# Turning two units a group through DRAM in a short attention branch, and moving six weight subtractions to GpSimd

## The chip, the cores and the metric

The kernel runs on one core of one Trainium2 chip. The metric is the device time of that core in microseconds (us) for one launch, the median of the runs shown. The engines are TensorE (PE in the profile, with PEld for its weight loads), VectorE (DVE), ScalarE (ACT), GpSimd (POOL) and SyncE (SP, which here only issues DMAs). Each takes its instructions in the order of its own queue and waits on semaphores for the others.

## The reference

One encoder layer runs over two sequences with the same weights: `x_sample` with 512 tokens and `x_prompt` with 1024, both 1024 wide, in float32. The token mixer has two branches that are merged by gates:

```python
z = xn @ w_in
qa, ka, va, qb, kb, vb, ga, gb = jnp.split(z, idx, axis=-1)
qa = _apply_rope(_rmsnorm(qa..., q_norm_g), cos, sin)      # 8 heads
ka = _apply_rope(_rmsnorm(ka..., k_norm_g), cos, sin)      # 2 key heads, 4 query heads each
o_a = _gqa_attention(qa, ka, va)                           # branch A: softmax(q k^T / 8) v, all tokens
o_b = _neighbourhood_attention(qb, kb, vb, rpb)            # branch B: windows of 8 x 16 tokens
merged = sigmoid(ga) * (o_a @ w_proj_a) + sigmoid(gb) * (o_b @ w_proj_b)
x = x + merged @ w_out
x = x + square(relu(rmsnorm(x) @ w_up)) @ w_down
```

A last RMS norm follows. The change touches branch A of the short sequence and the first weights of branch B of the long one.

## The kernel before

**Numbers in two parts.** Products are made in a float32 form that TensorE reads at one pass, and the lost precision is made up by splitting. A value is copied by ScalarE into a high part (`split`, line 203; `AF.Copy` into `F32R`), and the low part is the value less the high part, a subtraction (line 210) by the engine that `subtract[0]` names: VectorE, or GpSimd where it is set so. A product is then two or three matmuls (`mm3`, line 220).

**Order of the work.** `run` handles the short sequence first (`NB` = 1, `NT` = 4 tiles of 128 tokens), then the long one (`NB` = 2, `NT` = 8), then comes the MLP. Within a sequence: for each of two groups of four heads a phase R (projection, norm, rotation of q, k, v; tiles `z`, `zv`, `pq`) and a phase A (attention); then phase B (branch B), phase G (merge and output projection). The program is written in one order; a planner sorts each engine's queue from it by its own costs, and grants buffers as older tiles come free, so that the queues need not have the program's order.

**Phase A.** A unit is a head and a block of 512 queries; a short group has four units, a long one eight. For each 128 queries, `s_tile` makes the scores in PSUM (`s`, lines 810 and 811, pool `big` with two buffers), VectorE takes the maximum (line 813), and ScalarE the exponential (line 822) into `p`, queries on partitions. The product with the values needs keys on partitions, and there are two ways to turn `p`:
- On TensorE: `t_chunk` transposes four blocks of 128x128 into PSUM (`pT`, line 857); ScalarE makes the high part `pth` from PSUM (line 860) and VectorE the low part `ptl` (line 861).
- Through DRAM: the exponential is written with its columns permuted, VectorE transposes 32x32 blocks in place (line 875, `turn_a`), SP stores the tile (`ta`, line 876) and fetches it in quarters in the turned order (`hq`, `fetch_a`, line 901); ScalarE makes the high part (line 906) and GpSimd the low part in two halves (line 908, `cut_a`).

Before the change, the long sequence sends every second unit of a head (`qb` = 1) through DRAM; the short one transposes all units on TensorE. `pv` (lines 844 and 845) multiplies with the values, `LAG` = 2 chunks behind the turning; `finish_o` scales and stores the result.

**Filling.** `fill` holds matmuls of a gate (`gps`, 24 of them a column chunk, weights `w_g`) that are put between the attention's own by `fill.pull`. In the long sequence's phase A `subtract[0]` is GpSimd, and it is set back to VectorE at its end (line 974).

**Start of phase B.** `prep(0)` asks for the value strips and the bias; the gate 3328 is added to `fill` (line 1315); `load_qk(0)` (line 1316) loads and splits the first query and key weights (`w_bq`, `w_bk`); one pull (line 1317) starts the gate, which loads and splits its first chunk of weights; then `qkproj` (line 1318) multiplies (`pqb`, `pkb`).

Of the kernel before, what the change touches and what calls it, by code (L numbers as in the profile page):

```python
# [18 lines left out]
P = 128  # L19
# [42 lines left out]
def encoder(ctx: ExitStack, tc: tile.TileContext, xs, outs, w):  # L62
# [24 lines left out]
    def slot(shape, dt, name, left=False):  # L87
        return (s8l if left else s8r).tile(shape, dt, tag="s8", name=name)
# [336 lines left out]
    def run(tr, nxt, first):  # L425
# [120 lines left out]
        for g in range(2):  # L546
# [251 lines left out]
            with phase(f"phA{N}_{g}") as ph:  # L798
                units = [(h, qb) for h in range(4) for qb in range(NB)]
                PP, L4, rd = {}, {}, {}  # L800

                def s_tile(u, j):
                    h, qb = u
                    nm = f"{N}_{g}_{h}_{qb}_{j}"
# [48 lines left out]
                def t_chunk(u, kc):  # L853
                    h, qb = u
                    pt = mm(f"pT{N}_{g}_{h}_{qb}_{kc}")
                    for j in range(4):
                        nc.tensor.transpose(pt[:, j * P : (j + 1) * P], PP[u, j][:, kc * P : (kc + 1) * P], ident)
                    hi = ph.tile([P, 512], F32R, tag="pth", name=f"pth{N}_{g}_{h}_{qb}_{kc}", bufs=3)
                    lo = ph.tile([P, 512], F32R, tag="ptl", name=f"ptl{N}_{g}_{h}_{qb}_{kc}", bufs=3)
                    nc.scalar.activation(hi, pt, AF.Copy)  # L860
                    nc.vector.tensor_tensor(lo, pt, hi.bitcast(F32), op=ALU.subtract)
                    queue.append((u, kc, hi, lo))
# [25 lines left out]
                def fetch_a(u, i):  # L888
                    nm = f"{N}_{g}_{u[0]}_{i}"
                    if i < 3:  # L890
                        hl = slot([P, 2, 16, 64], F32R, f"hq{nm}")
                        hi, lo = hl[:, 0], hl[:, 1]
                    else:
                        hi, lo = (
                            ph.tile([P, T], F32, tag="P", name=f"hq{nm}_{e}", bufs=8)
                            .bitcast(F32R)
                            .rearrange("p (a w) -> p a w", w=64)
                            for e in range(2)
                        )
                    src = PD[u].rearrange("t (a i) (b w) -> i b (t a) w", i=32, b=4)[:, :, :, 64 * i : 64 * i + 64]  # L900
                    nc.sync.dma_start(lo.bitcast(F32), src)
                    quarter[u, i] = hi, lo

                def cut_a(u, i):
                    hi, lo = quarter[u, i]
                    nc.scalar.activation(hi, lo.bitcast(F32), AF.Copy)
                    for a in (slice(0, 8), slice(8, 16)):
                        nc.gpsimd.tensor_tensor(lo[:, a], lo[:, a].bitcast(F32), hi[:, a].bitcast(F32), op=ALU.subtract)

                if NB == 2:  # L910
                    subtract[0] = nc.gpsimd
# [6 lines left out]
                    for h in range(4):  # L918
# [15 lines left out]
                        for kc in range(NT):  # L934
# [6 lines left out]
                            hi, lo = (t[:, :, kc % 2 * 32 : kc % 2 * 32 + 32] for t in quarter[u, kc // 2])  # L941
                            queue.append((u, kc, hi, lo))
                            fill.pull(0 if kc in (1, 4) else 1)
                            next_pv()
                            if h < 3 and kc in (4, 6):
                                fetch_a(nd, kc // 2 - 2)
                else:
                    for j in range(4):
                        ends = s_tile(units[0], j)
                        last_exp[:] = [ends]  # L950
                        fill.pull(2)
                    for ui, u in enumerate(units):
                        h, qb = u
                        if first:
                            bias_row(g * 4 + ui)
                            if g == 0 and ui == 1:
                                early["a"] = load_a(1)
                            if g == 0 and ui == 2:
                                early["v"] = load_v(1, slot)
                        nxt_u = units[ui + 1] if ui + 1 < len(units) else None  # L960
                        sdone = 0
# [98 lines left out]
        with phase(f"phB{N}") as ph:  # L1060
# [1057 lines left out]
```

## Time and profile before

| | us |
|---|---|
| median of 3 runs | 2098.93 |
| lowest, highest run | 2098.87, 2101.75 |
| the profiled execution | 2099.86 |
| its span, first to last instruction | 2098.1 |

The profile is one execution. Its mean granted TensorE clock is 0.996. A row of a timeline gives the start, the time taken, the engine, the line, the operation, what is written and read, the shape, and in brackets the idle time ahead of it with what ended that. A row of a group or of a tile gives the shortest, the median and the longest in nanoseconds. In a row of windows, each engine's busy time is followed by its count of instructions; the last three numbers are the granted clock, the DMA engines' mean share and GB/s. Matmuls overlap, so a record's time (0.39 us for 512 columns) is longer than the spacing from one to the next.

### The profile page before, as it was taken

What the parts mean: (1) busy time and instruction counts of PE and PEld (TensorE: products, weight loads), DVE (VectorE), ACT (ScalarE), POOL (GpSimd) and SP (SyncE); (2) the same over time, 40 slices, a digit from 0 to 9 for tenths busy, and PEclk for the clock granted to TensorE, in tenths of its full rate; (3) what the DMA queues carried; (4) which work ended last, traced back from release to release, by engine and by line L of the source; (5) the groups of instructions that cost most, each with busy time, mean ns of one, the idle gap of its engine ahead of it and who ended that gap; (6) DMA issues with size and microseconds to landing.
All of it is one profiled execution on the core that took longest, in us unless ns stands there. A gap on an engine that the chain in (4) does not pass through costs nothing. (4 is left out here: it accounts for less than half of the span.)

```text
span 2098.1 us, 31227 instructions
## 1 busy us (share of the span) xinstructions
PE 2070.3 (99%) x10615; PEld 1815.6 (87%) x10615; DVE 1468.7 (70%) x2697; ACT 1142.8 (54%) x2455; POOL 441.3 (21%) x550
## 2 busy tenths in 40 slices
PE   9999999999999899999999999999999999999998
PEld 8888778888898788888888999999999988888887
DVE  6665786778458746778845777787777777669563
ACT  6674653668557735556413566565656634334442
POOL 2323310317725733453002000011000000000000
PEclk9999999999999999999999999999999999999999
DMA  6537557558528767776544556487445899688461
GB/s 194 148 111 207 158 163 256 186 147 228 152 67 230 197 169 206 218 243 200 192 170 155 182 188 210 145 252 208 149 157 161 284 339 350 214 279 279 151 210 62
DMA packets 407910, 409.99 MB, mean 195 GB/s; under 512 B 98367, under 2 KB 334919, under 8 KB 407751
## 3 DMA queue, kind: packets, MB, share of 16 engines
q1 hardware_dynamic: 368119, 339.16, 52.5%
q10 hardware_dynamic: 29408, 41.96, 5.9%
q0 software_dynamic: 10224, 26.88, 5.0%
q8 instruction: 84, 1.38, 0.3%
q14 instruction: 75, 0.61, 0.1%
HBM read 294.21 MB, written 114.49 MB: 195 GB/s over the span
## 5 line engine op out<-in xcount | busy, mean ns | idle before, releaser
L216 PE MATMUL dn<-wd,ah 128*128 128x512 f32 x1248 | 384.1, 389 | 0.0
L216 PEld LDWEIGHTS dn<-wd,ah 128*128 128x128 f32 x1248 | 234.2, 188 | 48.4
L216 PE MATMUL dn<-wd,al 128*128 128x512 f32 x624 | 242.8, 389 | 0.0
L1592 ACT ACTIVATE ah<-ar 128x512 fp32r<-128x512 f32 x168 | 104.6, 628 | 207.4 <-PE dn L216 198.1
L216 PE MATMUL gpss<-xs_0h,w_gs 128*128 128x512 f32 x512 | 186.6, 401 | 0.0
L1593 DVE TENSOR_TENSOR al<-ar,ah 128x512 fp32r<-128x512 f32 x168 | 114.6, 688 | 81.7 <-ACT ah L1592 69.2
L216 PE MATMUL ud<-B,A 128*128 128x384 f32 x768 | 145.0, 337 | 2.3 <-DVE c L1710 2.3
L216 PE MATMUL uc<-B,A 128*128 128x384 f32 x768 | 143.7, 334 | 0.0
L216 PE MATMUL ua<-B,A 128*128 128x384 f32 x768 | 139.1, 334 | 0.0
L216 PEld LDWEIGHTS dn<-wd,al 128*128 128x128 f32 x624 | 117.1, 188 | 24.5
L216 PEld LDWEIGHTS ud<-B,A 128*128 128x128 f32 x768 | 135.1, 189 | 2.6 <-DVE c L1710 2.6
L216 PEld LDWEIGHTS ua<-B,A 128*128 128x128 f32 x768 | 134.1, 188 | 0.2
L216 PEld LDWEIGHTS uc<-B,A 128*128 128x128 f32 x768 | 134.0, 188 | 0.2 <-ACT A L1592 0.2
L180 POOL TENSOR_TENSOR rs_f<-ms_f,mhalf 128x1 f32<-128x1 f32 x6 | 4.0, 667 | 590.7 <-DVE ms_f L176 590.7
L813 DVE TENSOR_REDUCE nms<-ss 128x1 f32<-128x1024 f32 (+1 forms) x96 | 99.3, 1037 | 32.2 <-PE ss L811 32.0
L216 PE MATMUL ops<-wh_os,mgs 128*128 128x512 f32 x384 | 119.5, 391 | 0.0
L822 ACT ACTIVATE ps<-ss,nms 128x1024 f32<-128x1024 f32 (+1 forms) x96 | 93.3, 973 | 37.4 <-DVE nms L813 36.3
L216 PEld LDWEIGHTS gpss<-xs_0h,w_gs 128*128 128x128 f32 x512 | 96.6, 189 | 17.8
L216 PE MATMUL gpss<-xs_0l,w_gs 128*128 128x512 f32 x256 | 101.4, 396 | 0.0
L1592 ACT ACTIVATE A<-S 128x512 fp32r<-128x512 f32 x128 | 75.8, 623 | 32.7 <-DVE S L1655 23.9
L216 PE MATMUL gpss<-xs_1h,w_gs 128*128 128x512 f32 x256 | 91.3, 395 | 0.4 <-ACT sgs L470 0.4
L1225 POOL TENSOR_SCALAR pbs<-pbs,rlbs 128x384 f32<-128x384 f32 (+1 forms) x96 | 71.7, 752 | 84.7 <-DVE rlbs L1224 70.4
(307 smaller groups left out, 5170.3 us busy)
## 6 DMA issues: line engine op xcount, KB each, us to landing
ar<-ud SPq DMA_DIRECT2D x120, 512.0 KB, 4.9
br<-in_w_mlp_down_dram SPq DMA_DIRECT2D x72, 512.0 KB, 5.4
rawu<-in_w_mlp_up_dram SPq DMA_DIRECT2D x64, 512.0 KB, 4.2
ud<-c ACTq DMA_DIRECT2D x128, 192.0 KB, 3.8
raw_gs<-in_w_in_dram SPq DMA_DIRECT2D x32, 512.0 KB, 3.9
tas<-ps SPq DMA_DIRECT2D x32, 512.0 KB, 3.7
hqs<-tas SPq DMA_DIRECT2D x32, 512.0 KB, 5.3
ud<-cs SPq DMA_DIRECT2D x64, 192.0 KB
```

The costliest lines, as they stand in the source:

```text
L180: op = nc.gpsimd.tensor_tensor(r[:, :n], m[:, :n], mhalf[:, :n], op=ALU.pow)
L216: op = nc.tensor.matmul(out, a, b, **kw)
L813: nc.vector.tensor_reduce(nm_, s, axis=AX.X, op=ALU.max, negate=True)
L822: op = nc.scalar.activation(to, of, AF.Exp, bias=nm_, accum_out=l)
L1225: nc.gpsimd.tensor_scalar(p, p, rl, 1.0, op0=ALU.mult, op1=ALU.mult)
L1592: nc.scalar.activation(hi, src, AF.Copy)
L1593: nc.vector.tensor_tensor(lo, src, hi.bitcast(F32), op=ALU.subtract)
```

## The change

The short branch A now sends heads 1 and 2 of each group through DRAM; heads 0 and 3 stay on TensorE. The scores of heads 1 and 0 are made first, then four loops follow in the order of heads 0, 1, 3, 2; the loops of heads 0 and 1 make the scores of heads 2 and 3. The gate's pulls are as many as before (24 a group), spread otherwise. The fetched tiles get two buffers of their own, and `pth` and `ptl` have two in place of three in the short branch. In the long sequence's phase B the subtractions of `load_qk(0)`, and of the gate's first chunk that the pull starts, go to GpSimd.

```diff
+                def turned(u):
+                    return u[1] == 1 if NB == 2 else u[0] in (1, 2)
...
-                    if NB == 2 and qb == 1:
+                    if turned(u):
                         to = p.rearrange("p (b k i) -> p k b i", b=4, i=32)
                         of = s.rearrange("p (k i b) -> p k b i", b=4, i=32)
...
-                    hi = ph.tile([P, 512], F32R, tag="pth", name=f"pth{N}_{g}_{h}_{qb}_{kc}", bufs=3)
-                    lo = ph.tile([P, 512], F32R, tag="ptl", name=f"ptl{N}_{g}_{h}_{qb}_{kc}", bufs=3)
+                    hi = ph.tile([P, 512], F32R, tag="pth", name=f"pth{N}_{g}_{h}_{qb}_{kc}", bufs=1 + NB)
+                    lo = ph.tile([P, 512], F32R, tag="ptl", name=f"ptl{N}_{g}_{h}_{qb}_{kc}", bufs=1 + NB)
...
-                    if u[1]:
+                    if turned(u):
                         due.append((u, j))
...
-                        hl = slot([P, 2, 16, 64], F32R, f"hq{nm}")
+                        dims = [P, 2, 16, 64]
+                        if NB == 2:
+                            hl = slot(dims, F32R, f"hq{nm}")
+                        else:
+                            hl = ph.tile(dims, F32R, tag="hq", name=f"hq{nm}", bufs=2)
...
+                def queue_d(u, kc):
+                    hi, lo = (t[:, :, kc % 2 * 32 : kc % 2 * 32 + 32] for t in quarter[u, kc // 2])
+                    queue.append((u, kc, hi, lo))
...
-                    for j in range(4):
-                        ends = s_tile(units[0], j)
-                        last_exp[:] = [ends]
-                        fill.pull(2)
-                    for ui, u in enumerate(units):
...
+                    for h in (1, 0):
+                        for j in range(4):
+                            last_exp[:] = [step_s((h, 0), j)]
+                            fill.pull(1)
+                    for i, (h, ahead) in enumerate(((0, 2), (1, 3), (3, None), (2, None))):
...
                         for kc in range(NT):
-                            t_chunk(u, kc)
-                            if nxt_u is not None:
-                                while sdone < 4 and kc >= (0, 0, 1, 2)[sdone]:
-                                    s_tile(nxt_u, sdone)
-                                    sdone += 1
-
+                            if h in (0, 3):
+                                t_chunk((h, 0), kc)
+                            if ahead is not None:
+                                step_s((ahead, 0), kc)
+                            if i == 0 and kc == 0:
+                                for e in range(2):
+                                    fetch_a((1, 0), e)
+                            if i == 2 and kc == 2:
+                                fetch_a((2, 0), 1)
+                            if (i, kc) in ((0, 2), (0, 3), (2, 2), (3, 0)):
+                                cut_a((1 + i // 2, 0), int((i, kc) in ((0, 3), (3, 0))))
+                            if h in (1, 2):
+                                queue_d((h, 0), kc)
                             fill.pull(1)
                             next_pv()
+                        if i == 1:
+                            fetch_a((2, 0), 0)
...
+            subtract[0] = nc.gpsimd if NB == 2 else nc.vector
             wqk = load_qk(0)
             fill.pull(1)
+            subtract[0] = nc.vector
```

More of the change, by code (lines that the diff above doesn't have):

```diff
@@ L940, in run @@
                                 step_s((h + 2, 1), kc // 7)
-                            hi, lo = (t[:, :, kc % 2 * 32 : kc % 2 * 32 + 32] for t in quarter[u, kc // 2])
-                            queue.append((u, kc, hi, lo))
+                            queue_d(u, kc)
                             fill.pull(0 if kc in (1, 4) else 1)
@@ L947, in run @@
                 else:
[L948 to L953 removed]
+                    for h in (1, 0):
[3 more added lines that the diff above has]
+                    for i, (h, ahead) in enumerate(((0, 2), (1, 3), (3, None), (2, None))):
                         if first:
[L955 to L956 removed]
+                            bias_row(g * 4 + i)
+                            if g == 0 and i == 1:
                                 early["a"] = load_a(1)
[L958 removed]
+                            if g == 0 and i == 2:
                                 early["v"] = load_v(1, slot)
[L960 to L961 removed]
                         for kc in range(NT):
[L963 to L967 removed]
+                            if h in (0, 3):
[11 more added lines that the diff above has]
+                                queue_d((h, 0), kc)
                             fill.pull(1)
                             next_pv()
+                        if i == 1:
+                            fetch_a((2, 0), 0)
                 fill.drain()
```

## The prediction

> **What bounds the kernel now.** I read the page first: the header and the busy times.
>
> ```profile
> span 2098.1 us, 31227 instructions
> PE 2070.3 (99%) x10615; PEld 1815.6 (87%) x10615; DVE 1468.7 (70%) x2697; ACT 1142.8 (54%) x2455; POOL 441.3 (21%) x550
> ```
>
> TensorE is busy for 2070.3 of 2098.1 us. So time is won only by taking instructions off TensorE or by closing one of its few gaps, 28 us in all, and work added to another engine is free until TensorE waits for it. The change touches two stages, so I asked next for each stage by windows: branch A of the short sequence (its two groups, from the first score product to the last product with the values), then the second group of branch A of the long one.
>
> ```profile
> 50.40:92.30 41.90, 41.73 (x212) 33.11 (x211) 32.96 (x61) 30.90 (x63) 10.86 (x17) 1.00 0.50 139
> 125.10:165.50 40.40, 40.40 (x209) 32.99 (x208) 31.16 (x55) 29.09 (x60) 10.71 (x18) 1.00 0.46 119
> 590.00:747.00 157.00, 151.23 (x798) 126.62 (x798) 109.35 (x155) 101.47 (x214) 77.72 (x86) 0.99 0.67 175
> ```
>
> The columns are the length, then PE, PEld, DVE, ACT, POOL, the granted clock and the DMA. The short groups have no gap: 82.1 of 82.3 us of TensorE. The long group has 5.8 us of gap, a fifth of the whole kernel's. The waits of TensorE name its cause, and the timeline shows where it lies (TensorE, then VectorE, GpSimd and ScalarE):
>
> ```profile
> PE pTs L857 <- DVE ptls L861: 5.4, 2, 4.2
> 725.64 0.40 PE L216 MATMUL gpss<-xs_0l,w_gs 128*128 128x512 f32 x1
> 727.26 0.66 PE L857 MATMUL pTs<-ident,ps 128*128 128x128 f32 x4 [1.23 <-DVE ptls L861]
> 734.38 0.88 PE L857 MATMUL pTs<-ident,ps 128*128 128x128 f32 x4 [4.18 <-DVE ptls L861]
> 735.48 0.63 PE L845 MATMUL os<-ptls,vhls 128*128 128x512 f32 x1
> 738.04 0.41 PE L844 MATMUL os<-pths,vhls 128*128 128x512 f32 x1
> 734.40:738.10 3.70, 3.70 (x12) 3.02 (x13) 2.92 (x5) 0.60 (x1) 0.00 (x0) 0.54 0.89 271
> 724.63 1.97 DVE L210 TENSOR_TENSOR w_bqs<-raw_bqs,w_bqs 128x512 fp32r<-128x512 f32 x1 [1.20 <-ACT w_bqs L203]
> 726.53 1.28 DVE L861 TENSOR_TENSOR ptls<-pTs,pths 128x512 fp32r<-128x512 f32 x2
> 727.73 5.39 DVE L210 TENSOR_TENSOR w_bqs<-raw_bqs,w_bqs 128x512 fp32r<-128x512 f32 x1
> 733.65 0.68 DVE L861 TENSOR_TENSOR ptls<-pTs,pths 128x512 fp32r<-128x512 f32 x1
> 724.73 1.32 POOL L499 TENSOR_TENSOR ot_As<-ot_As,rbs 64x512 f32<-64x512 f32 x1
> 726.90 2.53 POOL L908 TENSOR_TENSOR hqs<-hqs 128x512 fp32r<-128x512 f32 x2
> 730.07 2.49 POOL L908 TENSOR_TENSOR hqs<-hqs,hqs 128x512 fp32r<-128x512 f32 x2
> 726.40 1.06 ACT L203 ACTIVATE w_bks<-raw_bks 128x1024 fp32r<-128x1024 f32 x1
> 727.95 0.60 ACT L860 ACTIVATE pths<-pTs 128x512 fp32r<-128x512 f32 x1 [0.49 <-PE pTs L857]
> 747.19 0.39 PE L216 MATMUL pqbs<-xs_0h,w_bqs 128*128 128x512 f32 x1
> ```
>
> This is the core of the argument. A low part of long B's first weights on VectorE takes 5.39 us, where its sisters of the same shape take 0.68. It stands still from 727.73 until GpSimd's last subtraction ends at 732.56; the one at 724.63 likewise waits for GpSimd's 1.32 us. VectorE serves in order, so the eviction `ptls`, ready at about 728.6, runs at 733.65, and TensorE, which needs that bank for its next transposes, stands for 4.18 us. Two of the evictions at 726.53 run at normal speed while GpSimd works: their source is in PSUM.
>
> **Part 1: the low parts move to GpSimd.** Six subtractions go, two each for `w_bqs`, `w_bks` and the first chunk of gate 3328, because the pull that starts that gate lies between the two assignments. TensorE gets back the waits of 1.23 and 4.18. It also gets back what the lowered clock cost: at 0.54 granted, six matmuls from 735.48 to 738.04 take 2.56 us where six at 0.23 take 1.38, that is 1.2, and the two steps between 734.38 and 735.48 take 1.10 where 0.66 is usual, 0.4 more. Together 7.0 us.
>
> What is late next is ScalarE, which has no pause from 722 to 730: it makes the high parts of the same weights in between. With the bank free at 725.7 the transposes of 727.26 start at 725.9; their copy on ScalarE can start at 727.4, behind `w_bks`, and not at 727.95; the low part follows at about 728.1 to 728.8, and the transposes of 734.38 want its bank at about 728.6. I put 0.5 us for these small waits, so **part 1 gives 6.5**.
>
> On GpSimd the six cost 6 x 1.30 = 7.8 us, by the subtraction of the same shape, with both inputs in SBUF:
>
> ```profile
> L908 POOL TENSOR_TENSOR hqs<-hqs x48: 1269/1296/1319, 470.6 to 728.2; 128x512 fp32r<-128x512 f32 x48
> 740.40 1.28 POOL L499 TENSOR_TENSOR ot_As<-ot_As,rbs 64x512 f32<-64x512 f32 x1 [7.84 <-DVE ot_As L496]
> ```
>
> GpSimd pauses 7.84 us before 740.40, so they fit behind the quarters. `pqbs` starts at 747.19 - 6.5 = 740.7 and needs the first two, done by 732.6 + 2.6 = 735.2. If the planner puts all six in front of the last two pairs of subtractions, the last quarter is ready at 726.9 + 7.8 + 5.2 + 0.7 (a DMA issue) = 740.6, where its products want it at 746.2 - 7 = 739: about 1.5 us are lost. If the same cover fails wholly, part 1 gives nothing; there is no reason for it to cost anything, since the GpSimd work behind it, the scaling of `ot_As`, has its reader far away. Bounds: 0 to -7.0.
>
> **Part 2: two of four units a group in short A.** Off TensorE go 4 units x 4 chunks = 16 chunks of four transposes. Their price is in the spacing, not in the 274 ns that a record shows:
>
> ```profile
> 59.64 0.39 PE L216 MATMUL gpss<-xs_0l,w_gs 128*128 128x512 f32 x1
> 59.87 0.39 PE L216 MATMUL gpss<-xs_0h,w_gs 128*128 128x512 f32 x1
> 60.10 0.60 PE L857 MATMUL pTs<-ident,ps 128*128 128x128 f32 x4
> 60.46 0.48 PE L216 MATMUL gpss<-xs_0h,w_gs 128*128 128x512 f32 x1
> 60.77 0.42 PE L810 MATMUL ss<-kTs,qTs 128*128 128x512 f32 x1
> ```
>
> From 59.87 to 60.77 lie two matmuls at 0.23 and one chunk: 0.90 - 0.46 = 0.44 us. So 16 x 0.44 = 7.0 us leave TensorE; the products themselves remain, 32 of 512 columns.
>
> On the other engines, with the rows of the long branch, which does the same already:
>
> ```profile
> L861 DVE TENSOR_TENSOR ptls<-pTs,pths x96: 648/681/694, 59.8 to 736.0; 128x512 fp32r<-128x512 f32 x96
> L860 ACT ACTIVATE pths<-pTs x96: 579/598/626, 58.7 to 735.3; 128x512 fp32r<-128x512 f32 x96
> L875 DVE STREAM_TRANSPOSE ps<-ps x32: 1208/1235/1248, 449.7 to 703.1; 128x1024 f32<-128x1024 f32 x32
> L906 ACT ACTIVATE hqs<-hqs x32: 1050/1060/1083, 466.6 to 725.5; 128x1024 fp32r<-128x1024 f32 x32
> tas<-ps SPq DMA_DIRECT2D x32, 512.0 KB, 3.7
> hqs<-tas SPq DMA_DIRECT2D x32, 512.0 KB, 5.3
> ```
>
> VectorE loses 16 x 0.68 = 10.9 us and gains 16 transposes of half that width, about 0.62 each (an estimate, half of 1.235): 9.9. ScalarE loses 16 x 0.60 = 9.6 and gains 8 x 1.06 = 8.5. GpSimd gains 16 x 1.30 = 20.8. SP gains 16 stores and 8 fetches. VectorE then has 63 of the 78 us that remain of the two groups, 81%, where it had 64.1 of 82.3, 78%. So no engine takes the bound by its sum.
>
> What TensorE can wait for is the way through DRAM. From the last exponential of a unit: a transpose 0.6, a store at most 3.7 (half the size of that row), a fetch 5.3, a copy 1.06, two subtractions 2.6: 13.3 us. I laid the new order out at 0.23 us a matmul and 0.44 a chunk, from the group's first score product: eight score slots of 5 matmuls end at 9.1; the slots of the four loops end at 16.4, 22.8, 29.2 and 33.8. Unit 1's last tile is turned at about 6.8 and stored by 10.5; its first half is ready at about 19.5 and wanted, two slots behind, at about 20.5; its second is ready at about 22 and wanted at 24. Unit 2's last tile is turned at about 18.7; its first fetch starts at about 22.6 and is ready at 31.6, wanted at 32.2. Its second half waits for a buffer (two of tag hq), freed at 26.0, and is ready at 35.0, wanted at 35.2. So the second turned unit has no margin. At the front of a group, score tiles come every 1.14 us, while two PSUM buffers and the chain of products, maximum and exponential (50.66 to 52.73 before, 2.1 us) allow one in 1.05: no margin there either.
>
> For these I take 0.5 us a group at the front and 1.0 a group at the end, **3.0 in all**. The bounds are 0, and, with every trip uncovered, 4 x 13.3 = 53 for the trips. I take a value near 0 since the long branch pays next to nothing for 32 such fetches: its ScalarE waited for them in all
>
> ```profile
>   ACT hqs L906: 4.2, 4
> ```
>
> 4.2 us in 4 cases (who waited for the stored tiles), and TensorE never. Behind a waiting copy on ScalarE stand exponentials and `pths`; behind a waiting fetch on SP stand the raw weights. One smaller edit: two buffers in place of three for `pth` and `ptl` make a copy wait for the product two chunks back, which comes a slot of 1.6 us or more ahead of need, and I cost it at 0; if a copy waits nevertheless, it is for less than that slot, 16 chunks x 1.6 = 26 us at the very worst. **Part 2 gives 7.0 - 3.0 = 4.0.**
>
> **The sum.** -6.5 - 4.0 = -10.5 us against the profiled execution, which took 2099.86 (span 2098.1 and 1.8 around it): 2089.4. The median of the three runs is 2098.93, 0.9 below the profiled one, so I predict **2088.4**. About 0.2%, 4.2 us, is what a measurement can tell from no change; that line lies at 2094.7.
>
> **Rivals.**
> 1. *Short A's gain is eaten by GpSimd.* The weights' subtractions stay on VectorE there, and 16 new GpSimd subtractions of 1.30 come beside them, which is just what stopped VectorE at 727.73. The windows hold this many of them:
>
> ```profile
> 50.40:92.30 41.90, 9.32 (x16) 0.00 (x0) 1.00 0.50 139
> 125.10:165.50 40.40, 7.23 (x10) 0.00 (x0) 1.00 0.46 119
> ```
>
> (VectorE's share of line 210 alone). GpSimd's 20.8 us are 28% of the 75 us left; 26 x 0.28 = 7 meetings, each with half a pair of subtractions, 1.3 us: 9 us of VectorE, against 75 - 63 = 12 that it has free. Where that slack lies in the wrong place, TensorE waits for 7 to 11 us in place of my 3, and part 2 gives between nothing and a loss of 4. With part 1's 6.5 that is -6.5 to -2.5: 2092.4 to 2096.4. Chance 0.20. The Trainium skill, GPSIMD Engine Reference, section Specifications, states the rule: GpSimd shares its SBUF interfaces with VectorE, and contends with VectorE instructions that have two SBUF inputs. The rows at 724.63 and 727.73 agree; by it part 1 is right and part 2 is in danger.
> 2. *A new wait takes the place of part 1's*: GpSimd puts the weights ahead of the quarters, or ScalarE, full from 722 to 730, becomes the bound. Part 1 gives 0 to 3: 2092 to 2095. For it speaks that ScalarE has no pause there, against it the 7.84 us that GpSimd has. Chance 0.12.
> 3. *Slower:* the round trip of the turned units decides. From a TensorE wait of (13.5 + 4.2) / 4 = 4.4 us per turned unit the kernel is slower by over 0.2%; with half of 13.3 uncovered it is 4 x 6.65 = 27 lost and 13.5 won: 2112. SP's queue could do that, if a load that waits for a raw buffer stands ahead of a fetch. The long branch speaks against it. Chance 0.04.
>
> The forecast, both parts together 8 to 14 us, has 0.62; better than that 0.02.
>
> **How the numbers follow.** The forecast covers 2084.9 to 2091; its best end is both parts whole, -14.0. Rivals 1 and 2 reach 2096.4. From 2084.5 to 2096 lie about 0.62 + 0.18 + 0.12 (rival 1 but for its end, and rival 2). Faster by over 0.2%: the forecast, and most of rivals 1 and 2, 0.85. Within: 0.11. Slower: 0.04.
>
> **What would show it.** Part 1: no line-210 record over 2 us near the end of long A, no wait of `pTs` for `ptls` over 1 us, a granted clock of 1.00 there, and six GpSimd subtractions at line 210. Part 2: 64 transposes on `pTs` in the short groups in place of 128, groups of 37 to 39 us and not 41. Wrong would be: TensorE waits of over 1 us on `hqs` in the short groups, VectorE records at line 210 over 2 us beside GpSimd's line 908, or groups as long as before.

## The result: 30 us slower

| | before | after |
|---|---|---|
| median, us | 2099.93 (4 runs, 2098.87 to 2101.75) | 2130.45 (4 runs, 2129.89 to 2130.84) |
| the profiled execution, its span | 2099.86, 2098.1 | 2130.84, 2129.1 |
| mean granted clock | 0.996 | 0.988 |

The ratio after to before is 1.0145, 95% interval 1.013 to 1.0161. Forecast was 2088.4 with a range of 2084.5 to 2096.0: the direction is wrong, and the time lies 34 us above the range.

The page after, header and busy times, then the two short groups and the second group of long A by windows, with columns as before:

```profile
span 2129.1 us, 31181 instructions
PE 2077.2 (98%) x10551; PEld 1814.6 (85%) x10551; DVE 1466.4 (69%) x2691; ACT 1141.4 (54%) x2447; POOL 471.7 (22%) x572
```
```profile
50.50:116.40 65.90, 51.46 (x203) 39.92 (x202) 39.78 (x61) 31.06 (x59) 22.22 (x25) 0.82 0.62 164
145.20:195.70 50.50, 39.59 (x176) 30.11 (x174) 26.32 (x49) 26.03 (x53) 20.72 (x26) 0.93 0.64 166
...
660.80:777.60 116.80, 115.64 (x560) 92.09 (x559) 83.45 (x104) 82.74 (x132) 74.46 (x78) 1.00 0.77 204
```

TensorE is busy for longer than before although it has 64 instructions less; that is the lower clock. The short groups take 65.9 and 50.5 us where they took 41.9 and 40.4, with gaps of 14.4 and 10.9 us where there were 0.2 and none, and granted clocks of 0.82 and 0.93 where it was 1.00. The long group's row starts at its first score product and ends at the first product of long B: 116.80 us, where the same stretch before ran from 624.23 to 747.19, 122.96 us. So part 1 works, and the loss lies ahead of that stretch. TensorE's largest waits after:

```profile
PE os L848 <- POOL hqs L915: 14.6, 5, 5.9
PE os L847 <- ACT hqs L913: 8.1, 3, 3.2
...
PE gpss L216 <- ACT w_gs L203: 2.6, 1, 2.6
...
PE pqbs L216 <- ACT w_bqs L203: 1.7, 1, 1.7
```

The columns are the total, the number of waits and the longest, in us. The old wait of `pTs` for `ptls` (5.4) is gone. The first two rows, 22.7 us, are products of the short groups waiting for fetched quarters. (The changed file's lines are 3 to 7 higher here: 848 is the old 845, 913 and 915 the copy and low part of `cut_a`, 908 its fetch, 879 the store, 878 the block transpose.) Place by place, from the starts of the same TensorE instructions in both timelines:

| step | before | after | difference |
|---|---|---|---|
| first score product, short group 1 | 50.66 | 50.72 | +0.1 |
| first score product, short group 2 | 125.32 | 145.41 | +20.1 |
| first `pqb`, short B | 165.46 | 197.49 | +32.0 |
| first `ppa`, behind short B | 275.15 | 313.17 | +38.0 |
| first score product, long A's second group | 624.23 | 660.80 | +36.6 |
| first `pqb`, long B | 747.19 | 777.59 | +30.4 |

So 32 us are lost in the two short groups and what lies between, and 6 more in short B, which the change does not touch. Now the trips of heads 1 and 2 in group 1. SyncE's, GpSimd's and ScalarE's timelines after, then TensorE's:

```profile
58.41 11.73 SPq L879 DMA_DIRECT2D tas<-ps  x4
70.31 2.28 SPq L908 DMA_DIRECT2D hqs<-tas  x2
...
87.15 1.00 SPq L527 DMA_DIRECT2D rawkvs<-in_w_in_dram  x2
88.74 0.37 SPq L908 DMA_DIRECT2D hqs<-tas  x1
```
```profile
77.06 2.50 POOL L915 TENSOR_TENSOR hqs<-hqs 128x512 fp32r<-128x512 f32 x2 [0.55 <-ACT hqs L913]
82.75 0.66 POOL L844 DMA_DIRECT2D rbs<-rds  x1 [3.19 <-DMA rds<-rls]
83.42 2.49 POOL L915 TENSOR_TENSOR hqs<-hqs 128x512 fp32r<-128x512 f32 x2
```
```profile
101.19 0.60 ACT L470 ACTIVATE sgs<-gpss 128x512 f32<-128x512 f32 x1 [2.08 <-PE gpss L216]
...
103.31 1.04 ACT L913 ACTIVATE hqs<-hqs 128x1024 fp32r<-128x1024 f32 x1
```
```profile
77.02 0.50 PE L847 MATMUL os<-hqs,vhls 128*128 128x512 f32 x1 [2.17 <-ACT hqs L913]
...
79.61 0.79 PE L848 MATMUL os<-hqs,vhls 128*128 128x512 f32 x1 [1.32 <-POOL hqs L915]
...
85.97 0.64 PE L848 MATMUL os<-hqs,vhls 128*128 128x512 f32 x1 [3.21 <-POOL hqs L915]
...
90.04 0.80 PE L216 MATMUL gpss<-xs_0h,w_gs 128*128 128x512 f32 x1 [2.58 <-ACT w_gs L203]
...
104.40 0.80 PE L847 MATMUL os<-hqs,vhls 128*128 128x512 f32 x1 [3.25 <-ACT hqs L913]
```

The first SyncE row holds four stores. The first of them, at 58.41, is head 1's last; the other three are head 2's, and each waits for VectorE to turn its tile. Only behind them, at 70.31, come head 1's fetches, 11.9 us after its last store. The second half's low part is late for another reason: GpSimd stands for 3.19 us ahead of the broadcast of another head's sums (line 844), which was put in front of it. In group 2 the same broadcast (GpSimd at 175.61) stands ahead of the low part for which TensorE waits longest, 5.88 us up to 178.80.

Head 2's fetches, at 88.74 and 93.05, stand behind loads of raw weights (lines 527 and 249) that wait for buffers. But that is not what TensorE waits for at 104.40. The first of them landed 5.2 us after its issue, at 93.9, and ScalarE copied it at 103.31, 9 us later. On ScalarE's queue the copy stands behind the activation of a gate's products (`sgs`, line 470), which had to wait for the last gate product that TensorE did before its own wait, and behind two copies of raw weights. So by these rows a third in-order queue, ScalarE's, made this wait of 3.25 us. SyncE's own waits after, between 50 and 200 us:

```profile
SPq L879 <- DVE ps L878: 48.8, 12, 13.5
...
SPq L908 <- PE os L848: 11.8, 3, 5.0
...
SPq L527 <- DVE wgls L210: 8.0, 1, 8.0
```

For 48.8 us the queue stood at a store whose tile was not turned yet, with whatever was behind it. Some 27 us of that are the two waits for a group's first tile; what it cost the trips is the 11.9 us ahead of head 1's fetch in group 1 and 7.7 in group 2 (from the store at 153.10 to the fetch at 160.84). In the row of line 908 is head 2's first fetch of group 2, which stood 5.0 us, up to 180.58, until head 1's late products had freed one of the two buffers.

### The profile page after: what moved, and what is told of

The parts are those of the page before. It is cut to its first block, busy times and chain, and to the rows that moved or that the text cites. A ratio compares the mean times of both kernels' runs of the same rounds, so it can differ in the third digit from the quotient of the medians.

```text
span 2129.1 us, 31181 instructions
## 1 busy us (share of the span) xinstructions
PE 2077.2 (98%) x10551; PEld 1814.6 (85%) x10551; DVE 1466.4 (69%) x2691; ACT 1141.4 (54%) x2447; POOL 471.7 (22%) x572
## 5 line engine op out<-in xcount | busy, mean ns | idle before, releaser
L816 DVE TENSOR_REDUCE nms<-ss 128x1 f32<-128x1024 f32 (+1 forms) x96 | 99.1, 1033 | 24.1 <-PE ss L814 23.6
L1610 ACT ACTIVATE A<-S 128x512 fp32r<-128x512 f32 x128 | 75.9, 624 | 32.3 <-DVE S L1673 23.5
```

Source lines behind the costliest of these rows:

```text
L816: nc.vector.tensor_reduce(nm_, s, axis=AX.X, op=ALU.max, negate=True)
L1610: nc.scalar.activation(hi, src, AF.Copy)
```

## The experiments

My first theory was that the in-order queues of SyncE and GpSimd lengthen the trip. The rivals were that the trip is simply too long, that GpSimd stops VectorE, and that the smaller edits (buffers) do it. From the third run on, the edits touch only the short sequence, and part 1 stays in throughout.

**Each part alone.** e1_part1 is the kernel before with

```diff
+            subtract[0] = nc.gpsimd if NB == 2 else nc.vector
             wqk = load_qk(0)
             fill.pull(1)
+            subtract[0] = nc.vector
```

and e2_part2 the changed kernel without these two lines.

> The kernel before, with the six subtractions of the long branch B's first weights on GpSimd and nothing else. In the changed kernel the step from the long A's second group to the start of B took 6.2 us less than before (+36.57 us late at its scores, +30.40 at pqb). If the two parts do not meet, this runs 6 us faster than before (about 2093.5). If the changed kernel's later stage only got shorter because it came late, with its loads already there, this gains under 2 us.

> The changed kernel with the subtractions of load_qk(0) back on VectorE. All theories: the long A ends with its waits of about 5.5 us and the low clock again, so 6 to 7 us slower than the changed kernel, about 2137. Part 2 alone is then +37 us.

Measured: 2092.33 (9 runs), ratio 0.9963 [0.9952, 0.9974], and 2139.54 (4 runs), ratio 1.0181 [1.0156, 1.0206], beside 2100.72 for before. Part 1 gives 8.4, part 2 costs 38.8; the changed kernel has +30.5, so they add. In e1_part1 the stretch of long A's second group is 116.64 us (620.68 to 737.32), 6.3 less than before. The interval of the 8.4 is 5.5 to 10.1, so the 6.3 lie in it. In these two profiles the rest lies in short B (3 us, from its products to the first `ppa`), where part 1 changes nothing; no run here explains it. The six subtractions on GpSimd, by source line in the changed kernel:

```profile
L210 POOL TENSOR_TENSOR w_bqs<-raw_bqs,w_bqs x2: 1300/1306/1312, 767.5 to 768.7; 128x512 fp32r<-128x512 f32 x2
...
L210 POOL TENSOR_TENSOR w_gs<-raw_gs,w_gs x2: 1278/1282/1287, 774.9 to 776.2; 128x512 fp32r<-128x512 f32 x2
```

**One turned unit at a time.** The other unit is still turned and stored, but neither fetched nor copied; its products read arbitrary data that is ready early. (`cut_a` follows the fetches in these edits and is not shown.)

```diff
 e9_only_unit1
-                            if i == 2 and kc == 2:
-                                fetch_a((2, 0), 1)
...
-                        if i == 1:
-                            fetch_a((2, 0), 0)
...
+                            if h == 2:
+                                queue.append(((2, 0), kc, kT[:, 0, :], kT[:, 1, :]))
 e10_only_unit2
-                            if i == 0 and kc == 0:
-                                for e in range(2):
-                                    fetch_a((1, 0), e)
...
+                            if h == 1:
+                                queue.append(((1, 0), kc, kT[:, 0, :], kT[:, 1, :]))
```

> The changed kernel, but head 2 of each short group is turned and stored and neither fetched nor cut; its products read kT in its place. Theory of the queues (a fetch or a cut stands in its engine's queue behind instructions that wait for something else, and the second unit's fetch waits for the first unit's products to free its two buffers): unit 1's own waits stay, 2.3 + 1.6 + 3.8 us in the first group and 2.8 + 6.1 in the second, with 3 to 5 us of low clock; unit 2's go: 10 to 15 us less than the changed kernel, 2115 to 2120. Rival, the trip through DRAM is too long in itself: unit 2's share is the same as unit 1's, half of the 38 us, also 2110 to 2115. Rival, GpSimd stops VectorE: half of the cuts are left, half of the loss, 2110 to 2115.

> The changed kernel, but head 1 of each short group is turned and stored and neither fetched nor cut; its products read kT in its place, so that they never wait, and both buffers are free for head 2. Theory of the queues and the shared buffers: unit 2's fetch no longer waits for unit 1's late products, and all but 0 to 5 us of the 38 us go: 2090 to 2098. Rival, the trip through DRAM is too long in itself (13.3 us by the rows, no margin): unit 2 still waits, 8 to 15 us are left, 2100 to 2108. Rival, GpSimd stops VectorE: half of the cuts are left, 2110 to 2115.

Measured: 2114.1 and 2106.8 (one run each), 21.8 and 14.5 above part 1 alone; the sum, 36.3, is near the 38.1 of both. So both units are late, each mostly by itself. Both numbers missed my theory of the queues and lie where a rival put them: head 2 alone was to cost at most 5 us, for I had taken its lateness for that of the buffers it shares with head 1. By the totals a trip that is too long in itself fits better. The trace of e10 says otherwise for its first wait: the fetch is issued at 79.78, its data is copied only at 90.95, 11.2 us later (a fetch of this run lands in 5.8, the median), directly behind `sgs` (88.83) and two weight copies on ScalarE, and TensorE waits 3.24 us for it.

**The order of SyncE's queue, GpSimd's queue, and the buffers.** e5_fetch_first ties head 2's stores behind head 1's fetches; e6_no_rb_wait reads the reciprocal sums from a constant, so that the broadcast of line 844 waits for nothing (this leaves out the division by the sums); e12_pth3 gives `pth` and `ptl` their third buffer back.

```diff
 e5_fetch_first
-                    nc.sync.dma_start(PD[u][j], p)
+                    with tc.issue_after(fetched[-1]) if NB == 1 and h == 2 else nullcontext():
+                        nc.sync.dma_start(PD[u][j], p)
 e6_no_rb_wait
-                        src = rd.pop(u).rearrange(
+                        src = (rone if NB == 1 else rd.pop(u)).rearrange(
 e12_pth3 (likewise ptl)
-                    hi = ph.tile([P, 512], F32R, tag="pth", ..., bufs=1 + NB)
+                    hi = ph.tile([P, 512], F32R, tag="pth", ..., bufs=3)
```

> The changed kernel, but SP's stores of head 2 in a short group are queued behind both fetches of head 1. In the changed kernel's first group the last store of head 1 is issued at 58.41 and its first fetch at 70.31, behind three stores of head 2 that wait for VectorE. Theory of the queues: the fetch goes out at about 62 to 63, the waits for head 1's high part in the first group (2.3 us, and 1.6 behind it) go with their low clock; the second group, where the fetch stands behind one store only, stays: 4 to 7 us less than the changed kernel, 2123 to 2126. Rival, the trip is too long in itself (store, landing, fetch, landing): no gain, 2128 to 2132. Rival, GpSimd stops VectorE: no gain.

> The changed kernel, but the short branch's reciprocal sums are broadcast from a constant in DRAM, so that GpSimd's broadcast no longer waits for the sums' store to land; this leaves out the division by the sums. In the changed kernel GpSimd stood 3.2 us at that broadcast (up to 82.75 us) with head 1's second half cut by ScalarE at 79.6 and waiting behind it. Theory of the queues: the two waits of TensorE for head 1's low parts (3.8 and 6.1 us) shrink by 5 to 9 with their low clock: 2119 to 2125. Rival, GpSimd's subtractions are too slow or stop VectorE: no gain, 2128 to 2132.

> The changed kernel with three buffers for pth and ptl in the short branch, as before. ScalarE's copies waited 7.6 us in all for the products two chunks back. Theory of the queues: these waits stand behind TensorE's own waits for hq and cost nothing by themselves: within 3 us of the changed kernel, 2127 to 2133. Rival, the two buffers set TensorE's pace: 5 to 8 us less, 2122 to 2125.

Measured, one run each: 2124.4 (6.1 less than the changed kernel), 2120.9 (9.5 less) and 2130.6 (no change). All three lie in the range of the theory of the queues. The buffers of `pth` and `ptl` cost nothing, and e6 works as expected: the waits for GpSimd's low parts fall from 14.6 to 8.1 us. e5 has its number by luck. Its fetches are issued 7 us earlier and group 2 starts 11.8 us late, not 20.1, but the waits that were to go are still there (SyncE, ScalarE, then TensorE):

```profile
63.32 2.94 SPq L909 DMA_DIRECT2D hqs<-tas  x2
66.39 4.30 SPq L880 DMA_DIRECT2D tas<-ps  x3
```
```profile
77.83 2.01 ACT L914 ACTIVATE hqs<-hqs 128x1024 fp32r<-128x1024 f32 x2
```
```profile
78.94 0.51 PE L847 MATMUL os<-hqs,vhls 128*128 128x512 f32 x1 [3.47 <-ACT hqs L914]
...
82.99 0.79 PE L848 MATMUL os<-hqs,vhls 128*128 128x512 f32 x1 [3.21 <-POOL hqs L916]
```

With the 4.6 us that a fetch takes to land in this run (median), the first half lay ready at about 68 (an estimate), and ScalarE copied it at 77.83, behind exponentials and copies of raw weights. What went is the wait of `gps` for its weights (2.6 us at 90.04 in the changed kernel), and how the rest of the 6.1 came about no run here shows.

**GpSimd taken off the turned units.** e11_one_late (on part 1) turns only head 1 and multiplies it last, so that the trip is covered, with GpSimd still making the low parts; `fetch_a` and `cut_a` of head 2 go, and head 1's `cut_a` comes later; that is not shown. e13_one_late_dve is the same with VectorE making them, e4_cut_dve the changed kernel with VectorE making them, and e14_first_dve that with e5's order too.

```diff
 e11_one_late
-                    return u[1] == 1 if NB == 2 else u[0] in (1, 2)
+                    return u[1] == 1 if NB == 2 else u[0] == 1
...
+                    for i, (h, ahead) in enumerate(((0, 2), (2, 3), (3, None), (1, None))):
 e13_one_late_dve, e4_cut_dve, e14_first_dve
-                        nc.gpsimd.tensor_tensor(lo[:, a], ...)
+                        (nc.gpsimd if NB == 2 else nc.vector).tensor_tensor(lo[:, a], ...)
```

> Part 1, and in each short group only head 1 through DRAM, its scores first and its products last, behind heads 0, 2 and 3: some 15 us of room for the trip. 8 chunks of transposes leave TensorE, 8 x 0.44 = 3.5 us. Theory of the queues and of too little room: TensorE waits for hq under 2 us, and the kernel is 1 to 4 us faster than part 1 alone (which was 8 us under before): 2088 to 2092 against a before of 2100. Rival, a trip costs what the run with head 1 alone showed (+21.8 us over part 1 alone): 2110 or more.

> Part 1, and one turned unit a group whose products come last (as in e11_one_late), with the low parts of its fetched quarters made by VectorE and not by GpSimd. Theory 'GpSimd stopped VectorE there' (the low part of a gate weight at 80.06 took 5.86 us beside four of GpSimd's subtractions, and TensorE stood 7.2 us for the eviction behind it): the wait of pT for ptl goes, no record of line 210 is over 1 us in the short groups, and the time is 2098 to 2104, which leaves the late loads at short B. Rival 'VectorE was only short of time there' (the order of its queue, not GpSimd): 8 more subtractions of 0.68 us on VectorE a unit make it no better, 2109 to 2114.

> The changed kernel with the low parts of the short branch's fetched quarters made by VectorE and not by GpSimd. If GpSimd's part (its order, with the second half of a quarter's low part behind the broadcast of the sums, and its stopping of VectorE) is about half of the loss: 2112 to 2120, with no record of line 210 over 1 us in the short groups and no wait of TensorE of over 3 us for GpSimd. If only SyncE's order and the length of the trip decide: 2127 to 2132.

> Both cures in one: head 2's stores behind head 1's fetches (e5_fetch_first, 6 us) and the low parts on VectorE (e4_cut_dve). If the two are separate causes, the gains add: 6 us below e4_cut_dve, 2105 to 2114. If they are one chain, in which each only shows the other, it comes out within 2 us of the better of the two. In no case below part 1 alone (2092.3), since head 2's trip and the late loads at short B stay.

e11_one_late took 2111.43 (4 runs), ratio 1.0055 [1.0037, 1.0072], far over what I had expected and, by the total, where the rival put it. Its waits for `hqs` are down to 1.8 us, but another is there: VectorE's, GpSimd's and TensorE's timelines, then the window that follows the wait:

```profile
78.35 7.57 DVE L210 TENSOR_TENSOR w_gs<-raw_gs,w_gs 128x512 fp32r<-128x512 f32 x2
...
85.85 1.28 DVE L864 TENSOR_TENSOR ptls<-pTs,pths 128x512 fp32r<-128x512 f32 x2
...
80.45 4.92 POOL L915 TENSOR_TENSOR hqs<-hqs 128x512 fp32r<-128x512 f32 x4
...
86.58 0.90 PE L860 MATMUL pTs<-ident,ps 128*128 128x128 f32 x3 [7.23 <-DVE ptls L864]
```
```profile
86.50:90.00 3.50, 3.42 (x13) 2.94 (x14) 1.61 (x5) 1.33 (x3) 0.61 (x1) 0.50 0.79 251
```

Two low parts of a gate weight take 7.57 us on VectorE beside four of GpSimd's subtractions in a row: the second, at 80.06, takes 5.86 alone and ends at 85.92, after GpSimd's fourth at 85.37. TensorE stands for 7.23 us for the eviction behind it, and then runs at a clock of 0.50. That is the stall which part 1 cures in the long branch, made again in the short one.

e13_one_late_dve took 2108.89 (4 runs), ratio 1.0042 [1.0025, 1.0059]: above what the GpSimd theory said, a little below what its rival said. The 5.86 us record is gone, the wait fell from 7.2 to 2.0, and group 2 starts 4.3 us earlier than in e11 (130.42 against 134.71). Of this, 2.5 are left in the medians, whose intervals overlap; TensorE now waits 3.3 us for `w_bqs` at short B. So the stall is shown, and it was worth some 4 us where it happened, not the 7 to 13 that the theory asked for. e4_cut_dve took 2110.0, 20.5 less than the changed kernel and better than either theory said. Line 210 on VectorE by groups, 50 to 166 us, in the changed kernel and then in e4_cut_dve (busy, mean ns):

```profile
L210 DVE TENSOR_TENSOR wgls<-rawqs,wghs 128x512 fp32r<-128x512 f32 x4 | 6.2, 1593 | 0.5 <-ACT wghs L203 0.5
L210 DVE TENSOR_TENSOR wl_vs<-raw_vs,wh_vs 128x512 fp32r<-128x512 f32 x4 | 6.0, 1550 | 1.0 <-ACT wh_vs L203 1.0
```
```profile
L210 DVE TENSOR_TENSOR wl_vs<-raw_vs,wh_vs 128x512 fp32r<-128x512 f32 x4 | 2.5, 686 | 0.0
L210 DVE TENSOR_TENSOR wgls<-rawqs,wghs 128x512 fp32r<-128x512 f32 x4 | 2.5, 685 | 0.0
```

GpSimd cost VectorE 7.2 us in these eight. Of the 20.5, e6 puts 9.5 down to GpSimd's queue; if the two add, the other 11 are the stops and GpSimd's slower pace (2.5 us a pair, VectorE 1.29) together, and no run tells these two apart. e14_first_dve took 2108.2, 1.8 below e4 (one run each): the gains of e4 and e5 don't add. Its trace shows why for head 1 in group 1. The fetch is issued at 63.55 and not at 71.49, but ScalarE's copy runs at 78.22 (77.09 in e4), and TensorE waits for it 3.45 us (2.17 in e4).

**The stores off SyncE's queue.** e15_pool_stores is e4_cut_dve, and e16_one_pool_stores is e13_one_late_dve, with the short branch's stores issued by GpSimd.

```diff
-                    nc.sync.dma_start(PD[u][j], p)
+                    (nc.sync if NB == 2 else nc.gpsimd).dma_start(PD[u][j], p)
```

> As e4_cut_dve (low parts on VectorE), and the stores of the turned tiles are issued from GpSimd's queue and not SyncE's, so that no store that waits for VectorE stands ahead of a fetch, and the value strips' loads for short B move up. If what is left in e4_cut_dve (10 us above before, 17.7 above part 1 alone) is SyncE's order: TensorE's waits for ScalarE's copy of head 1's fetched quarter and for w_bq go or fall under 1 us, and the time is 2096 to 2104. If it is the bare length of the trip (store, fetch, copy, two low parts, 13 us and more against the products' slots), the waits stay, within 2.5 us of e4_cut_dve: 2107.5 to 2112.5.

> As e13_one_late_dve (one turned unit a group, its products last, low parts on VectorE), with the stores issued from GpSimd's queue. e13 has hardly a wait left for fetched quarters, so the trip is covered; what it loses lies at 80 to 87 (evictions behind the weights on VectorE, 5.9 us) and at short B (w_bq late, 3.3, and the score stage, 4.7). If the late loads there are SyncE's order: 2099 to 2105. If they come from the buffers and the DMA engines, it stays at 2107 to 2111. Under part 1 alone (2092.3) only if all of it goes.

Measured: 2107.12 (6 runs), ratio 1.0039 [1.0027, 1.0052], and 2096.19 (10 runs), ratio 0.9987 [0.9978, 0.9996]. e16 is 12.7 us faster than e13 with nothing changed but the queue that issues eight stores. Of this 9.0 are there by the first `ppa` (279.51, in e13 288.47): TensorE's waits in short B for loads and scores, not for quarters, are what went. Taken by the total, e15 goes to the rival, 2.9 below e4; its trace says otherwise. SyncE issues head 1's fetches at 62.28 and not at 71.49 as in e4. TensorE's waits, then what SyncE did before short B:

```profile
PE pqbs L216 <- ACT w_bqs L203: 6.4, 1, 6.4
PE os L847 <- ACT hqs L913: 2.5, 2, 2.1
PE pTs L860 <- DVE ptls L864: 2.1, 1, 2.1
PE os L848 <- DVE hqs L915: 1.9, 2, 1.1
```
```profile
157.77 3.36 SPq L908 DMA_DIRECT2D hqs<-tas  x2
161.18 15.56 SPq L1110 DMA_DIRECT2D vss<-vds  x16
176.78 0.43 SPq L249 DMA_DIRECT2D raw_bqs<-in_w_in_dram  x1
```

The waits for quarters fell from 9.9 us in e4 (8.1 and 1.8) to 4.4; head 1's copy in group 1 now runs at 68.91, and TensorE waits for it no more, as SyncE's order would have it. But the wait for the first weights of short B grew from 4.2 to 6.4, and one of 2.1 for `ptls` and two for scores (1.5) came. These weights are asked for at 176.78, behind sixteen strip loads that stand behind the last fetches. In the kernel before, the strips went out inside group 2 and the same load came at 144.32, 21 us ahead of its use:

```profile
144.32 0.40 SPq L249 DMA_DIRECT2D raw_bqs<-in_w_in_dram  x1
```

**The weights ahead of the strips.** e17_two_w_first is e15, e18_one_w_first is e16, and e19_part1_w_first is part 1 alone, with this exchange in the short sequence:

```diff
-            prep(0)
+            if NB == 2:
+                prep(0)
             fill.add(gate(3328, zg[1]))
...
             subtract[0] = nc.vector
+            if NB == 1:
+                prep(0)
```

> As e15_pool_stores, with the first weights of short B asked for ahead of the value strips and bias of its first heads (in the program's order, for the short sequence alone). In e15 the load of raw_bq is issued at 176.78, behind sixteen strip loads that take SyncE 15.56 us, and TensorE waits 6.4 us for w_bq. If SyncE's order alone makes that wait: the load goes up by 10 us or more, the wait goes, and the time is 2098 to 2102 (6.4 us and about 1.5 of low clock). If the strips are then late in turn (a new wait at short B's products): 2104 to 2108.

> As e16_one_pool_stores with the same exchange. There the waits for w_bq are 1.8 and 1.0 us and the lost time at the start of short B 4.9. If SyncE's order makes them: 2090 to 2093, about level with part 1 alone (0.9963 of before, within 0.0015). If the loads wait for buffers or for the DMA engines: 2095 to 2097.

> The control: part 1 alone with the same exchange. There raw_bq is loaded 21 us ahead of its use already, so the exchange by itself should give nothing: within 2 us of part 1 alone (ratio 0.9952 to 0.9974). Under 0.995 the exchange is a gain of its own, and what e18 shows is not of the turned units.

Measured: 2100.63 (10 runs), ratio 1.0002 [0.9992, 1.0012]; 2094.2 (10 runs), 0.9971 [0.996, 0.9982]; and 2092.22 (4 runs), 0.9961 [0.9946, 0.9976]. In e17 the load is issued at 160.76, the wait for `w_bqs` is gone, and 6.5 us with it. e18 is 2.0 below e16, less than SyncE's order alone was to give, and their intervals overlap. The control moves nothing. So with two turned units the loss against part 1 alone went down step by step: 38.1 as changed (2130.45 less 2092.33), 17.6 with GpSimd off the low parts (one run), 14.8 with the stores off SyncE, 8.3 with the weights ahead. What is left in e17 is waits for quarters and evictions (the latter 2.1 us, as in e15). The quarters' are again ScalarE's queue: head 2's fetches of group 2 are issued at 157.35 and 160.35, and with 5.6 us to land (median of this run) both lay ready by about 166 (an estimate), but the copies stand behind `sgs`:

```profile
PE os L848 <- DVE hqs L915: 3.0, 2, 1.9
PE os L847 <- ACT hqs L913: 2.5, 2, 2.1
```
```profile
168.46 0.60 ACT L470 ACTIVATE sgs<-gpss 128x512 f32<-128x512 f32 x1 [2.08 <-PE gpss L216]
169.46 2.00 ACT L913 ACTIVATE hqs<-hqs 128x1024 fp32r<-128x1024 f32 x2 [0.40 <-ACT sgs L470]
```

No run puts these copies ahead of `sgs`, so what that would give is not shown. No order with turned units came under part 1 alone, which at 2092.3 is the best version found (2092.2 with the weights ahead); e18's interval overlaps its own.

## Why the prediction was wrong, step by step

**Part 1: right.** Forecast 6.5; 6.3 measured alone and 6.2 in the changed kernel, over the same stretch. No wait of `pTs` is left there, the clock is 1.00, and the six cost GpSimd 1.28 to 1.31 each (1.30 forecast). Rival 2, a new wait in its place, did not come; one of 1.1 us for ScalarE's `pths` appeared earlier in the stretch (at 701.59 in e1, 741.87 in the changed kernel), which was in neither the forecast nor the kernel before.

**Part 2, the 7.0 us of transposes:** half of them are gone, 64 fewer instructions on TensorE, as forecast. Their worth was not measured apart from the waits.

**Part 2, "3.0 in all" for the waits: this step failed.** If the transposes gave their 7.0, part 2's cost of 38.8 alone means 45.8 us where 3.0 was put. TensorE's waits for quarters (14.6 and 8.1), gate weights (2.6) and short B's first weights (1.7) are 27.0 of it; the other 19 I put down to the lowered clock and to short B; they were not measured one by one. The bounds that I gave, 0 to 53, held it; the value taken in them did not. The trip's own durations were right. Group 1, us after the first score product:

| head 1 | forecast | after | e5_fetch_first | e15_pool_stores |
|---|---|---|---|---|
| last tile turned | 6.8 | 7.6 | 7.6 | 7.6 |
| fetch issued | 10.5 | 19.6 | 12.6 | 11.6 |
| first half's low part done | 19.5 | 28.8 | 32.3 | 23.7 |
| products wanted (forecast) or wait from | 20.5 | 24.1 | 24.8 | no wait for this half |

From the fetch to the low part the trip took 9.2 us after, against 9.0 forecast. It is 9.3 late, and 9.1 of that it was late already when the fetch was issued. Without a store ahead, the fetch goes out 8.0 earlier (last column), so these are SyncE's queue. But the low part then comes 5.1 earlier, and in e5 it comes 3.5 later, because the other queues take over: ScalarE's copy stands behind exponentials and weight copies, and the low part behind what VectorE or GpSimd has ahead of it. I had laid out when the data would be ready and not what stands ahead on each queue that fetches, copies and subtracts it, although the prediction names SyncE's and ScalarE's. Head 2 was worse: first fetch forecast at 22.6, issued at 38.0 (88.74).

The evidence behind "near 0", that the long branch pays next to nothing, was no evidence for this place. It is the same trip with the same durations (stores of twice the size landed in 3.7 us before, these in 3.9; fetches in 5.3 and 5.2), but what is ahead of each fetch on SyncE, of each copy on ScalarE and of each low part on GpSimd differs by stage.

Not in the sum at all were: GpSimd's wait for the sums' broadcast ahead of a low part (9.5 us by e6), what the stage after pays (1.7 us of wait for its first weights and the 6 us of short B here; in e15 the loads pushed back on SyncE cost 6.5, by e17), and the clock after each wait. In this window of the changed kernel TensorE is busy all the time and yet does seven products and four transposes, 2.1 us of work at the prediction's 0.23 and 0.44 (the 11 of the row), in 4.00:

```profile
90.00:94.00 4.00, 3.96 (x11) 2.94 (x12) 3.11 (x5) 0.60 (x1) 1.36 (x3) 0.50 1.21 217
```

**Rival 1** (GpSimd stops VectorE; 9 us of VectorE time) had the size right, 7.2 us over eight records, and TensorE's price too low: 7 to 11 us of waits, where taking GpSimd off the low parts (e4, one run) gave 20.5, its queue included. The Trainium skill's rule (GPSIMD Engine Reference, Specifications: contention with VectorE instructions that have two SBUF inputs) agrees with e11's row: 5.86 us for one such instruction.

**Rival 3**, slower by the round trip, is what came, and dearer: 27 us lost in its forecast of 2112, 45.8 measured. Its picture, a load that waits for a raw buffer ahead of a fetch, stands in SyncE's rows (8.0 us at line 527, then the fetch at 88.74), but that fetch had landed 9 us before its copy ran; ahead of head 1's fetch stood the other head's stores, and GpSimd's and ScalarE's queues did the rest. A chance of 0.04 was far too low for a layout whose second turned unit, by the prediction itself, "has no margin".

**The small edits:** two buffers for `pth` and `ptl` cost nothing (e12, 2130.6, one run). The front of a group costs 0.2 us in all (TensorE's waits of `ss`), where 1.0 was put.

## What to carry to other kernels

A moved step is as long as its queues, so write down for each new DMA what is ahead of it on its issuing queue and what that waits for, do the same for each copy and subtraction on its engine's queue, and for each old DMA what is now ahead of it. A store that waits for its data holds every fetch and load behind it, and an early fetch gains nothing while its copy stands behind something else (e5, e14). That the same construction is free in another stage says nothing until these neighbours are compared. When a cure changes the total little, read whether its own wait went before calling the theory wrong: in e15 head 1's went, and others grew. And when a run gives the forecast number, read whether the wait that was to go did go: in e5 it did not.

## What the runs showed of the hardware

A wait of TensorE of 2.04 us was followed by half the clock. Two windows of e13_one_late_dve, the first with the wait at its end, the second right behind it:

```profile
79.00:81.50 2.50, 0.51 (x2) 0.19 (x1) 2.50 (x4) 2.04 (x4) 1.29 (x2) 0.96 1.09 307
81.50:84.00 2.50, 2.45 (x9) 2.14 (x10) 2.50 (x5) 0.90 (x1) 0.00 (x0) 0.50 1.06 387
```

So a wait's price is more than its length: the 2.5 us at 0.50 hold three products and six transposes, 1.4 us of work at the prediction's spacing. GpSimd doesn't slow VectorE's two-input subtraction evenly; it held one through two or more of its own instructions (5.86 us beside four of them in e11, 3.39 beside two, the longest in the changed kernel, 0.68 undisturbed). And to issue a fetch can take long by itself. SyncE's records of the fetches after, shortest, median and longest in ns:

```profile
L908 SPq DMA_DIRECT2D hqs<-tas x8: 366/416/5689, 70.3 to 183.4; - x8
```

The one of 5.69 us, at 161.57, held the store behind it, whose tile VectorE had turned by 162.8, until 167.35. In e4 the same fetch took 5.92 us, and in e15, where no such store is on SyncE's queue, the longest took 1.30; what made it so long no run here shows.
